# Unread products in front of four waits of TensorE in a one-core decoder layer

## Chip, cores and metric

The kernel runs on one core of a Trainium2 chip. The metric is the device time of one execution in microseconds (us). An engine's busy time, waits and the clock granted to TensorE (1.00 is the full 2.4 GHz, 0.50 is 1.2 GHz) come from one profiled execution.

## What is computed

One decoder layer on x of 512 tokens by 1024, float32. Two head groups read one combined projection; their outputs go through one output projection, then a LayerNorm, a routed mixture of experts and a second LayerNorm:

```python
def reference(x, w_in, ...):
    h = x
    p = h @ w_in
    p_rwkv, p_moba = p[..., :RWKV_COLS], p[..., RWKV_COLS:]
    p_prev = jnp.pad(p_rwkv[:, :-1], ((0, 0), (1, 0), (0, 0)))
    p_rwkv = p_rwkv + (p_prev - p_rwkv) * mu_shift
    p_r, p_k, p_v, p_wd, p_ad, p_gd = _split(p_rwkv, RWKV_SPLITS)
    y_a = _rwkv7_group(p_r, p_k, p_v, p_wd, p_ad, p_gd, ...)   # 8 recurrent heads x 64, delta rule
    q_m, k_m, v_m = _split(p_moba, MOBA_SPLITS)
    y_b = _moba_group(q_m, k_m, v_m)                            # 8 heads x 64, block-sparse attention
    mix = jnp.concatenate([y_a, y_b], axis=-1) @ w_out
    h = _layer_norm(DEEPNORM_ALPHA * h + mix, ln1_g, ln1_b)
    ffn = _hier_moe(h, ...)     # 4 groups, best 1; its 8 experts, best 2; SwiGLU, width 256
    h = _layer_norm(DEEPNORM_ALPHA * h + ffn, ln2_g, ln2_b)
```

## The kernel before

The engines are TensorE (PE; its weight loads are PEld), VectorE (DVE), ScalarE (ACT), GpSimdE (POOL) and SyncE (SP), which issues most loads. The code is written in stages; a scheduler sets each engine's order from priorities and estimated times, and each engine then runs its list strictly in that order. Where `strict[0]` is set, every product of TensorE is bound behind the one written before it; `last[1]` holds the product behind which the next ones are bound, `last[0]` the latest one written. `mm` (line 229) and `tp` (line 232) issue every product and transpose of TensorE, so nearly all its work bears one of these two lines, and is told apart by its banks (`bank0` to `bank7`, the eight accumulators; in the orders below `bank_64` to `bank_71`) and shapes. A float32 product of which both sides are full float32 shows as two pieces in the trace.

**Recurrent heads, 0 to 300 us.** The eight heads are worked in four pairs. For pair `hp`, `feat` makes the features. Its three projections (`proj`, of K, R and V) are 24 products of 128x512 each over hi and lo parts of x and of the weights; `split_w` makes these parts on ScalarE (line 336) and on VectorE or GpSimdE (line 337). Between K and R the norm of K is taken: four products with `hsel` into `pn`, the inverse root on VectorE and GpSimdE (`rsqrt`, lines 239 to 247, the last step on ScalarE), then four transposes into `pi`, which VectorE L441 reads. R is evacuated by L348 (ScalarE) and L349 (VectorE) and multiplied by GpSimdE L464; V is evacuated by L471 and L472. `pre` builds the pair's chunk matrices: its products of 128x128 need L464's result; VectorE masks them (lines 565 to 573) and solves a triangular system by 15 rounds of shuffle, product and sum (L578, L579, L580), after which TensorE goes on (`both`). `feat(1)` is woven into `pre(0)` by priority, and so on.

**Routing, about 430 to 490 us.** Token blocks 3 to 0 of 128 tokens are routed in an order written out by hand (`MODE`): output projection, transposes, logits, choice of experts (`picks`), position in the expert's list (`rank`: products of the blocks' masks, into bank 6), norm. `rows0` gathers the rows of the first expert pair with products of one-hot masks (128x128); then come `slots_of` (tables of places), `ups(0)` (32 products of the first pair's up weights), `gates_of` (the gate values, 128x32, for which VectorE and GpSimdE compute lines 1068 to 1086) and `read_gates`. `gains1` (lines 1007 and 1012) applies the LayerNorm's gain and bias on GpSimdE and VectorE beside it. SyncE stores the routing tables (line 1281) and behind that issues the next expert weights.

**Experts, about 490 to 755 us.** 32 experts are worked in 16 pairs (`experts_first`, `last_pair`), 64 rows each: `ups`, `hidden`, `turn`, `down`. Pairs 0 to 12 write to DRAM; from pair 13 (`LATE_`) on, `combine` adds the result to the tokens with one-hot products. Weights come through seven large and six small buffers; a load is issued when its buffer comes free. After the last pair comes the second LayerNorm.

Of the kernel before, what the change touches and what calls it, by code (L numbers as in the profile page):

```python
# [10 lines left out]
BF = mybir.dt.bfloat16  # L11
# [160 lines left out]
def v3(ap, a):  # L172
    return ap.rearrange("p (a b) -> p a b", a=a)
# [12 lines left out]
def layer(ctx: ExitStack, tc: tile.TileContext, xT, xt, wb, wad, pc, wla, al, gl, cst, cst2, cst3, abias, wout,  # L186
# [7 lines left out]
    B = [pps.tile([128, 512], F32, name=f"bank{i}") for i in range(8)]  # L194
# [9 lines left out]
    def bank(ids):  # L204
        k = rot.get(ids, 0)
        rot[ids] = k + 1
        return B[ids[k % len(ids)]]
# [4 lines left out]
    last = [None, None]  # L212
# [5 lines left out]
    strict = [False]  # L218
# [9 lines left out]
    def mm(o, l, r, start=True, stop=True):  # L228
        return inorder(PE.matmul(o, l, r, start=start, stop=stop, skip_group_check=True))  # L229

    def tp(o, i):
        return inorder(PE.transpose(o, i, late("ident")))  # L232

# [3 lines left out]
    def rsqrt(out, y, x, t):  # L237

        V.tensor_scalar(t.bitcast(I32), x.bitcast(I32), 1, None, op0=OP.logical_shift_right)
        V.tensor_scalar(y.bitcast(I32), t.bitcast(I32), -1.0, float(0x5F3759DF), op0=OP.mult, op1=OP.add)  # L240
        P.tensor_scalar(x, x, -0.5, None, op0=OP.mult)
        for j in range(3):
            P.tensor_tensor(t, y, y, op=OP.mult)
            P.tensor_tensor(t, t, x, op=OP.mult)
            P.tensor_scalar(t, t, 1.5, None, op0=OP.add)
            P.tensor_tensor(y, t, y, op=OP.mult)
        S.activation(v3(out, 8), y[:, :, None].to_broadcast([128, 8, 64]), AF.Copy)  # L247
# [151 lines left out]
    def feat(hp, fill=()):  # L399
# [34 lines left out]
        nx = T(24)  # L434
        V.tensor_scalar(nx.f[:, 0:8], pn[:, 0:8], 1e-24, None, op0=OP.max)
        rsqrt(kkn.f, nx.f[:, 8:16], nx.f[:, 0:8], nx.f[:, 16:24])
        pi = bank(LB)
        for i in range(4):
            tp(pi[:, 128 * i:128 * i + 128], kkn.f[:, 128 * i:128 * i + 128])
        nx.free()  # L440
        V.scalar_tensor_tensor(kkn.f, k.f, pcol(f"kk{hp}"), pi, op0=OP.mult, op1=OP.mult)  # L441
        at("fe", hp)
# [599 lines left out]

    def rank(i, lg4, mx, oo, gg, og, gm, ww, ww8, ex4, e2, gs, m4, r1, rr):
        prk = B[RKB][:, 0:32]
        for j in range(3, i, -1):
            mm(prk, onesb, mb[:, j, :], start=(j == 3), stop=False)
        mm(prk, trisb, mb[:, i, :], start=(i == 3))
        V.scalar_tensor_tensor(r1, v3(prk, 4), 1.0, m4, op0=OP.add, op1=OP.mult)
        V.tensor_reduce(rr[:, 0:8], r1.rearrange("p g e -> p e g"), axis=AX.X, op=OP.add)
        for e in range(2):  # L1050
            ins = V.tensor_scalar(OHP[i].f[:, 64 * e:64 * e + 64], late("iota64"), rr[:, e:e + 1], og[:, 0:1],
                                  op0=OP.is_equal, op1=OP.mult)
        placed[0] = ins
        return lg4, mx, oo, gg, og, gm, ww, ww8, ex4, e2, gs
# [95 lines left out]
    def ups(p, ht, ph):  # L1150

        for k in range(8):
            for e in range(2):
                ins = mm(ph[64 * e:64 * e + 64, :], v3(ht.f, 8)[:, k, 64 * e:64 * e + 64],
                   wa_[2 * p + e][:, 512 * k:512 * k + 512], start=(k == 0), stop=(k == 7))
        return ins
# [3 lines left out]
        gates(i, *kept[i], part=1)  # L1160

    strict[0], last[1] = True, ins
    ins = ups(0, HT, B[0])
    strict[0], last[1] = False, None
    for i in range(3, -1, -1):
        gates_of(i, rrs[i], OHt[i], ins)
# [109 lines left out]
    def experts_first():  # L1276


        for i in range(4):
            gains1(i, (P, V), True, (0,) if f"g{i}" in MODE else range(2))  # L1280
        after(SP.dma_start(rdram, RR.f), g1, "rows first")
        BB[6] = area("b6")
        GA.append(T(1024, BB[6]))
        HTs.append(T(1024, BB[6]))
        P.memset(GA[1].f, 0.0)
        gather(2)
        strict[0], last[1] = True, last[0]

        def second(p):
            Y = YY[p % 2]  # L1290
            for n in range(2):
                py = B[4 + n]
                down(p, n, py)
                if n:
                    V.tensor_copy(Y.g[:, 512:1024], py)
                else:
                    S.activation(Y.g[:, 0:512], py, AF.Copy)
            P.indirect_dma_start(out=ydram, out_offset=bass.IndirectOffsetOnAxis(ap=IDY.i[:, p:p + 1], axis=0),  # L1298
                                 in_=Y.g, in_offset=None, bounds_check=1023, oob_is_err=False)
            loads_b(p)  # L1300

        for p in range(15):
            ph = B[6] if p % 2 and p < LATE_ else B[0]
            if p:
                ups(p, HTs[p % 2], ph)
            if p == 13:
                L2.append(area(f"a{SA[4]}"))
                G2 = T(2048, L2[0])
                for j in range(2):
                    SP.dma_start(G2.f[:, 1024 * j:1024 * j + 1024], lnp[2 + j:3 + j, :].to_broadcast([128, 1024]))  # L1310
                P.tensor_scalar(G2.f[:, 0:1024], G2.f[:, 0:1024], -12.0 * K_ ** 5, None, op0=OP.mult)
                L2.append(G2)
            late_a = []
            if p < HP:
                load_pair(2 * p + 7, 7)
            for e in range(2 * p + 7, min(2 * p + 9, 2 * LQ) if p >= HP else 0):
                if p < 4 or e == 2 * p + 7:
                    load_a(e, SA)
                else:
                    late_a.append(e)  # L1320
            hidden(p, ph)
            if p < LATE_:
                rows(p + 1, dst=HTs[(p + 1) % 2])
                if p + 3 < 16:
                    gather(p + 3)
                if p > 0:
                    second(p - 1)
                if p == LQ - 3:
                    load_pair(2 * LQ, 0)
                turn(B[3])  # L1330
            else:
                cbs = lambda k: combine(p - 1, CBS[k]) if p > LATE_ else None
                if p == LATE_:
                    second(p - 1)
                    combining()
                    back()
                cbs(0)
                turn(B[3])
                cbs(1)
                py = bank((4, 5))  # L1340
                down(p, 0, py)
                parts(0, py)
                cbs(2)
                rows(p + 1, (0,), HTs[(p + 1) % 2])
                cbs(3)
                rows(p + 1, (1,), HTs[(p + 1) % 2])
                if p + 3 < 16:
                    gather(p + 3)
                ot(p)
                py = bank((4, 5))  # L1350
                down(p, 1, py)
                parts(1, py)
            for e in late_a:
                load_a(e, SA)
        gained_rows()
        last_pair(SB, None)
# [253 lines left out]
```

## Time and profile before

| | |
|---|---|
| median of 3 runs | 757.5 us (754.66 to 757.62) |
| the profiled execution | 756.99 us, span 754.9 us |
| mean granted clock of TensorE | 0.931 |
| busy: TensorE, VectorE, ScalarE, GpSimdE | 87%, 48%, 36%, 28% |
| bytes moved | 147.18 MB |

The span runs from the first to the last instruction; some 2 us of the profiled execution lie outside it. A row of work by time gives start, busy time, engine, line, operation, what is written and read, shapes and count, and in brackets the idle time of the engine ahead of it with what ended that time. A busy TensorE is not TensorE at its peak.

### The profile page before, as it was taken

To read this page: it belongs to the slowest core of one execution; us is meant where nothing else is said; L and a number is where in the kernel's file an instruction comes from. 1 tells how busy PE (TensorE), PEld (TensorE's weight loads), DVE (VectorE), ACT (ScalarE), POOL (GpSimd) and SP (SyncE) were. 2 spreads that over 40 slices of the span, in tenths; PEclk is the share of its full clock that TensorE was granted. 3 is DMA by queue.
4 is the path that set the end of the run, shared out by engine and by line. 5 is a ranking of instruction groups with operands and counts; after the bars stand their busy time and mean duration, and the time that the engine had idled before them with its cause. 6 is when DMAs were issued, how large, how long until landed. Compare 5 with 4: busy or idle time off the path is not lost.

```text
span 754.9 us, 9697 instructions
## 1 busy us (share of the span) xinstructions
PE 660.1 (87%) x3420; PEld 416.7 (55%) x3420; DVE 359.1 (48%) x1091; ACT 273.0 (36%) x581; POOL 211.4 (28%) x302
## 2 busy tenths in 40 slices
PE   8879999889998997979999997599999897779780
PEld 3757887688777876845675676333334232323240
DVE  4277258415841585236445587922121121103975
ACT  4344543544274444536424532223131131101330
POOL 4233553445345533110000041721111111101432
PEclk9979999999999999998989997899999998988985
DMA  9611011001100110465440467499999999999503
GB/s 327 233 56 57 29 56 57 28 29 57 57 29 28 53 46 1 140 238 173 156 158 38 153 237 282 165 358 420 423 426 423 425 421 425 425 417 410 227 2 115
DMA packets 28484, 147.18 MB, mean 195 GB/s; under 512 B 5114, under 2 KB 5626, under 8 KB 20493
## 3 DMA queue, kind: packets, MB, share of 16 engines
q1 hardware_dynamic: 23676, 134.61, 45.5%
q0 software_dynamic: 4608, 11.62, 3.9%
q8 instruction: 29, 0.48, 0.3%
q10 hardware_dynamic: 144, 0.26, 0.1%
q14 instruction: 27, 0.21, 0.1%
HBM read 138.38 MB, written 15.36 MB: 204 GB/s over the span
## 4 chain that ended last, share of the span: by engine, by line
PE 30%; DMA 18%; DVE 8%; POOL 2%; issue 1%; ACT 0%; SPq 0%; DVEq 0%; POOLq 0%; ACTq 0%
PE bank L229 26%; DMA b<-in_wex 17%; PE bank L232 4%; DVE a L147 2%; DVE base L1375 1%; DMA b<-hdram,base 1%; DVE x L1075 1%; DVE base L1204 1%; DVE base L147 1%; POOL base L1007 0%; DVE base L778 0%; POOL base L1012 0%; DVE a L1431 0%; DVE x L1226 0%; POOL x L1086 0%
## 5 line engine op out<-in xcount | busy, mean ns | idle before, releaser
L229 PE MATMUL bank<-a,b 128*128 128x512 f32 (+2 forms) x1112 | 308.7, 467 | 14.9 <-DMA a<-in_wex 12.3
L229 PEld LDWEIGHTS bank<-a,b 128*128 128x128 f32 (+1 forms) x1112 | 159.7, 177 | 94.7 <-issue 47.2
L229 PE MATMUL bank<-b,base 128*64 128x512 f32 (+1 forms) x412 | 93.4, 497 | 8.6 <-DMA b<-in_wex 6.9
L229 PE MATMUL bank<-a,base 128*64 128x512 f32 (+3 forms) x308 | 73.5, 560 | 1.2 <-DMA a<-in_wex 0.8
L337 POOL TENSOR_TENSOR b<-b,b 128x1024 fp32r<-128x1024 f32 x22 | 52.3, 2376 | 73.6 <-ACT b L336 64.6
L229 PEld LDWEIGHTS bank<-b,base 128*64 128x64 f32 (+1 forms) x412 | 42.4, 161 | 49.5 <-issue 34.2
L229 PE MATMUL bank<-a 128*128 128x128 f32 (+6 forms) x264 | 62.7, 370 | 7.2 <-ACT a L627 3.8
L1209 DVE SCALAR_TENSOR_TENSOR base<-bank,base 128x256 f32<-128x256 f32 x16 | 7.7, 483 | 116.9 <-ACT base L1208 116.9
L1208 ACT ACTIVATE base<-bank 128x256 f32<-128x256 f32 x16 | 6.1, 384 | 121.8 <-PE bank L229 121.8
L229 PEld LDWEIGHTS bank<-a 128*128 128x128 f32 (+2 forms) x264 | 37.9, 200 | 20.6 <-issue 6.1
L229 PEld LDWEIGHTS bank<-a,base 128*64 128x64 f32 (+2 forms) x308 | 27.3, 140 | 39.0 <-issue 27.2
L229 PE MATMUL bank<-a,a 128*128 128x128 f32 (+2 forms) x200 | 43.2, 334 | 2.1 <-POOL a L464 2.1
L232 PE MATMUL bank<-base,a 128*128 128x128 f32 x152 | 33.1, 298 | 9.5 <-ACT a L247 7.8
L229 PEld LDWEIGHTS bank<-a,a 128*128 128x128 f32 x200 | 33.2, 202 | 9.5 <-issue 3.7
L229 PE MATMUL bank<-base 128*128 128x36 f32 (+4 forms) x136 | 30.2, 365 | 6.7 <-DVE base L1040 3.3
L336 ACT ACTIVATE b<-b 128x1024 fp32r<-128x1024 f32 x25 | 26.3, 1057 | 26.1 <-PE bank L229 18.7
L232 PE MATMUL bank<-base 128*128 128x128 f32 x156 | 31.1, 302 | 5.1 <-DVE base L1209 3.9
L232 PEld LDWEIGHTS bank<-base 128*128 128x128 f32 x156 | 19.0, 149 | 27.9 <-issue 16.3
L232 PEld LDWEIGHTS bank<-base,a 128*128 128x128 f32 x152 | 19.3, 148 | 22.4 <-ACT a L247 8.9
L229 PE MATMUL bank<-b,a 128*128 128x128 f32 x192 | 31.4, 276 | 0.2 <-DVE a L633 0.2
L229 PEld LDWEIGHTS bank<-b,a 128*128 128x128 f32 x192 | 29.9, 191 | 2.7 <-DVE a L633 0.4
L1298 POOL DMA_INDIRECT ydram<-x,base x13 | 13.1, 1008 | 63.9 <-ACT base L1214 34.6
(302 smaller groups left out, 960.5 us busy)
## 6 DMA issues: line engine op xcount, KB each, us to landing
a<-in_wex SPq DMA_DIRECT2D x28, 2048.0 KB, 24.0
b<-in_wex SPq DMA_DIRECT2D x30, 1024.0 KB, 26.4
b<-in_wb SPq DMA_DIRECT2D x25, 512.0 KB, 3.3
a<-in_wex SPq DMA_DIRECT2D x16, 512.0 KB, 15.7
ydram<-base SPq DMA_DIRECT2D x1, 4096.0 KB, 15.1
a<-ydram POOLq DMA_DIRECT2D x4, 1024.0 KB, 16.0
x<-in_wout SPq DMA_DIRECT2D x6, 512.0 KB, 4.3
a<-in_xT SPq DMA_DIRECT2D x8, 256.0 KB, 5.0
```

Source lines behind the costliest of these rows:

```text
L147: ins = f(*args, **kw)
L229: return inorder(PE.matmul(o, l, r, start=start, stop=stop, skip_group_check=True))
L232: return inorder(PE.transpose(o, i, late("ident")))
L336: S.activation(hi.f, raw.f, AF.Copy)
L337: (V if 0 < k < 4 else P).tensor_tensor(lo.f, raw.f, hi.g, op=OP.subtract)
L1075: V.scalar_tensor_tensor(ww[:, :, 0], ww[:, :, 0], gs, og, op0=OP.mult, op1=OP.mult)
L1204: V.scalar_tensor_tensor(hb[:, i, ns], hb[:, i, ns], 1.0, pc_, op0=OP.mult, op1=OP.add, accum_out=SUM.f[:, 2 * i + n:2 * i + n + 1] if p = ...
L1208: S.activation(hd.f, ph[:, 0:256], AF.Silu)
L1209: V.scalar_tensor_tensor(hd.f, ph[:, 256:512], GT.f[:, p:p + 1], hd.f, op0=OP.mult, op1=OP.mult)
L1298: P.indirect_dma_start(out=ydram, out_offset=bass.IndirectOffsetOnAxis(ap=IDY.i[:, p:p + 1], axis=0), in_=Y.g, in_offset=None, bounds_chec ...
L1375: E.tensor_tensor(h, h, RT[i].f[:, 1024 * r + 512 * n:1024 * r + 512 * n + 512], op=OP.add)
```

## The change

A helper `keep(n, o)` issues n products of 128x128 by 128x512 in bf16, read from two constants (the identity and a ramp, taken as bf16 bits), into a bank whose content nobody needs at that time. Nothing reads the result. It is called at four places: ahead of the four transposes of the first pair of heads (8 products, bank 6), ahead of the rank products of token block 0 (9, bank 5), behind `ups(0)` and ahead of the gate products (14, bank 7), and in expert pair 13 behind `turn` and ahead of `down` (16, bank 7). At the first two places the products, and what is written behind them up to the transposes or the rank product, are also bound into the written order.

```diff
+    def keep(n, o):
+
+        for _ in range(n):
+            ins = mm(o, late("ident").bitcast(BF)[:, 0:128], late("iota512").bitcast(BF)[:, 0:512])
+        return ins
+
...
         rsqrt(kkn.f, nx.f[:, 8:16], nx.f[:, 0:8], nx.f[:, 16:24])
+        if hp == 0:
+            strict[0], last[1] = True, last[0]
+            keep(8, B[6])
         pi = bank(LB)
         for i in range(4):
             tp(pi[:, 128 * i:128 * i + 128], kkn.f[:, 128 * i:128 * i + 128])
+        strict[0], last[1] = False, None
         nx.free()
...
         prk = B[RKB][:, 0:32]
+        if i == 0:
+            strict[0], last[1] = True, last[0]
+            keep(9, B[5])
         for j in range(3, i, -1):
             mm(prk, onesb, mb[:, j, :], start=(j == 3), stop=False)
         mm(prk, trisb, mb[:, i, :], start=(i == 3))
+        strict[0], last[1] = False, None
...
     strict[0], last[1] = True, ins
-    ins = ups(0, HT, B[0])
+    ups(0, HT, B[0])
+    ins = keep(14, B[7])
     strict[0], last[1] = False, None
...
                 cbs(1)
+                if p == 13:
+                    keep(16, B[7])
                 py = bank((4, 5))
                 down(p, 0, py)
```

The scheduler places the new products, and moves other work with them. On TensorE in the first pair of heads, from the four norm products (128x2, into `bank_67`) to the four transposes (line 232, into `bank_66`), there stood before:

```order
L229 MATMUL bank_67<-x_88,a_1_77 128x2 x4
L229 MATMUL bank_64<-a_1_74,b_1_81 128x512 x2
L229 MATMUL bank_67<-x_88,a_1_77 128x130 x2
L229 MATMUL bank_64<-a_1_75,b_1_81 128x512
L229 MATMUL bank_64<-a_1_74,b_1_81 128x512 x2
L229 MATMUL bank_64<-a_1_75,b_1_81 128x512
L229 MATMUL bank_64<-a_1_74,b_1_81 128x512 x2
L229 MATMUL bank_64<-a_1_75,b_1_81 128x512
L229 MATMUL bank_64<-a_1_74,b_1_81 128x512
L232 MATMUL bank_66<-base,a_1_77 128x128 x4
```

Now the eight unread products (into `bank_70`, each with its weight load) stand behind the norm products; from the last of them on the list reads as follows (the transposes are now line 238):

```order
L229 LDWEIGHTS base
L229 MATMUL bank_70<-base 128x512
L229 MATMUL bank_67<-x_88,a_1_77 128x130 x2
L229 MATMUL bank_64<-a_1_74,b_1_81 128x512 x2
L238 MATMUL bank_66<-base,a_1_77 128x128 x4
L229 MATMUL bank_64<-a_1_75,b_1_81 128x512
L229 MATMUL bank_64<-a_1_74,b_1_81 128x512 x2
L229 MATMUL bank_64<-a_1_75,b_1_81 128x512
L229 MATMUL bank_64<-a_1_74,b_1_81 128x512
L229 MATMUL bank_66<-x_88,a_1_77 128x130 x2
```

Of the ten products of R (into `bank_64`) ahead of the transposes, eight moved behind them. On VectorE in the same pair, from the last masks of `pre(0)` to the rounds of the solution, there stood before (L568, L572 and L573 are masks, L472 and L476 belong to V):

```order
L572 TENSOR_TENSOR b_1_84<-bank_70,x_88 128x4x64
L578 STREAM_SHUFFLE base<-base 128x8x15
L579 TENSOR_TENSOR base<-base 128x8x15
L580 TENSOR_TENSOR base<-base 128x8x15
...
L580 TENSOR_TENSOR base<-base 128x8x13
L568 TENSOR_TENSOR base<-bank_68,x_88 128x512
L472 SCALAR_TENSOR_TENSOR a_1_78<-bank_65,base,a_1_77 128x8x64
L573 TENSOR_TENSOR b_1_84<-bank_68,x_88 128x4x64
L476 TENSOR_TENSOR a_1_78<-bank_67,a_1_78 128x512
L578 STREAM_SHUFFLE base<-base 128x8x12
```

and now (the lines' numbers are ten higher from line 472 on: L482 is V's evacuation, L578 and L583 are masks, L588 to L590 a round):

```order
L482 SCALAR_TENSOR_TENSOR a_1_78<-bank_65,base,a_1_77 128x8x64
L578 TENSOR_TENSOR a_1_80<-bank_70,x_88 128x512
L486 TENSOR_TENSOR a_1_78<-bank_67,a_1_78 128x512
L578 TENSOR_TENSOR base<-bank_68,x_88 128x512
L582 TENSOR_TENSOR b_1_84<-bank_70,x_88 128x4x64
L583 TENSOR_TENSOR b_1_84<-bank_68,x_88 128x4x64
L588 STREAM_SHUFFLE base<-base 128x8x15
L589 TENSOR_TENSOR base<-base 128x8x15
L590 TENSOR_TENSOR base<-base 128x8x15
```

V's evacuation moved from behind the third round to ahead of the first. On TensorE in the routing, from the second half of the last logits (128x36) to the rank product of block 0 (the fourth 128x32, into `bank_70`), there stood before:

```order
L229 MATMUL bank_71<-base 128x36 x4
L229 LDWEIGHTS base
L229 MATMUL bank_70<-base 128x32
...
L229 MATMUL bank_66<-x_2753,base 128x128 x2
L229 MATMUL bank_67<-x_2753,base 128x128 x4
L229 LDWEIGHTS base
L229 MATMUL bank_70<-base 128x32
```

and now, with nine unread products into `bank_69` between the first two kinds:

```order
L229 MATMUL bank_71<-base 128x36 x4
L229 LDWEIGHTS base
L229 MATMUL bank_69<-base 128x512
...
L229 LDWEIGHTS base
L229 MATMUL bank_70<-base 128x32
L229 MATMUL bank_66<-x_2761,base 128x128 x2
```

The six gather products (into `bank_66` and `bank_67`) moved from ahead of the rank product to behind it. At the third and fourth places nothing but the new products moved on TensorE. Around 472 to 490 us VectorE and GpSimdE also take the steps of the gates and gains in a slightly other order: one gain step of VectorE (line 1007) comes ahead of its work on the gathered rows, and GpSimdE takes its first L1084 after two gain steps instead of three.

## Rows read from the trace of the kernel before

**Rows 1.** The chain that ended last, in order of time: start, us, what.

```profile
553.69 30.05 DMA b<-in_wex
...
650.08 31.91 DMA b<-in_wex
682.03 3.28 PE bank L229 x6
```

**Rows 2.** TensorE's work by time, 24 to 60 us.

```profile
23.89 6.64 PE L229 MATMUL bank<-a,b 128*128 128x512 f32 x28
...
36.25 1.12 PE L232 MATMUL bank<-base,a 128*128 128x128 f32 x4 [1.97 <-ACT a L247]
37.02 1.63 PE L229 MATMUL bank<-a,b 128*128 128x512 f32 x3
...
43.56 1.22 PE L229 MATMUL bank<-a,a 128*128 128x128 f32 x4 [2.13 <-POOL a L464]
...
52.22 6.89 PE L229 MATMUL bank<-a,b 128*128 128x512 f32 x22 [2.52 <-DVE b L337]
```

**Rows 3.** Windows: us, busy PE PEld DVE ACT POOL (counts), clock, DMA share, GB/s.

```profile
36.00:37.00 1.00, 0.75 (x4) 0.75 (x5) 0.00 (x0) 0.20 (x1) 0.00 (x0) 0.63 0.00 0
...
53.00:54.00 1.00, 1.00 (x5) 0.77 (x4) 1.00 (x4) 0.00 (x0) 0.00 (x0) 0.66 0.76 246
```

**Rows 4.** TensorE's work by time, the kernel's first products.

```profile
1.44 4.34 PE L229 MATMUL bank<-base 128*128 128x512 bf16 x10 [1.44 <-DVE base L321]
```

**Rows 5.** GpSimdE's and VectorE's work by time, 28 to 62 us.

```profile
41.81 1.70 POOL L464 TENSOR_TENSOR a<-a 128x512 f32<-128x512 f32 x1
...
48.91 3.25 DVE L337 TENSOR_TENSOR b<-b,b 128x1024 fp32r<-128x1024 f32 x1
...
58.43 0.27 DVE L580 TENSOR_TENSOR base<-base 128x104 f32<-128x104 f32 x1
...
60.72 0.75 DVE L472 SCALAR_TENSOR_TENSOR a<-bank,base,a 128x512 f32<-128x512 f32 x1
```

**Rows 6.** VectorE's and TensorE's work by time, 74 to 92 us.

```profile
74.29 0.17 DVE L580 TENSOR_TENSOR base<-base 128x8 f32<-128x8 f32 x1
...
85.16 1.16 PE L229 MATMUL bank<-a 128*128 128x128 f32 x8 [1.58 <-ACT a L627]
```

**Rows 7.** TensorE's work by time, 455 to 474 us.

```profile
467.01 2.89 PE L229 MATMUL bank<-x,base 128*128 128x128 f32 x12
469.71 0.20 PE L229 MATMUL bank<-base 128*128 128x32 bf16 x1
...
471.79 2.02 PE L229 MATMUL bank<-x,base 128*128 128x128 f32 x16 [1.24 <-DVE x L920]
```

**Rows 8.** Windows in the routing.

```profile
459.00:460.00 1.00, 1.00 (x8) 1.00 (x8) 1.00 (x4) 0.00 (x0) 0.00 (x0) 0.75 1.03 442
...
469.00:470.00 1.00, 0.92 (x6) 0.77 (x5) 0.55 (x5) 0.00 (x0) 0.00 (x0) 0.63 0.50 184
```

**Rows 9.** All engines' work by time, 474 to 500 us.

```profile
475.67 4.74 DVE L1075 SCALAR_TENSOR_TENSOR x<-x 128x4 f32<-128x4 f32 x1
...
476.63 2.52 POOL L1007 TENSOR_TENSOR base<-base,b 128x512 f32<-128x512 f32 x2
...
489.07 0.37 PE L229 MATMUL bank<-x 128*128 128x32 bf16 x8 [7.57 <-POOL x L1084]
489.18 0.33 SPq L1281 DMA_DIRECT2D rdram<-x  x1
```

**Rows 10.** A window behind the second pair's up products.

```profile
499.00:500.00 1.00, 0.68 (x4) 0.00 (x0) 0.00 (x0) 0.25 (x1) 0.00 (x0) 1.00 0.37 140
```

**Rows 11.** TensorE's work by time, 655 to 760 us.

```profile
678.60 1.94 PE L229 MATMUL bank<-b,base 128*64 128x512 f32 x2 [5.39 <-DMA b<-in_wex]
682.03 3.28 PE L229 MATMUL bank<-b,base 128*64 128x512 f32 x6 [1.49 <-DMA b<-in_wex]
```

**Rows 12.** A window behind the fourth place.

```profile
684.00:685.00 1.00, 1.00 (x3) 0.02 (x1) 0.00 (x0) 0.00 (x0) 1.00 (x3) 0.61 1.07 414
```

## The prediction

> **What bounds the kernel now.** I read four views in this order: the page's table of engines, the chain that ended last, TensorE's work by time, and the granted clock in windows of 1 us. TensorE is the busiest engine, so a reader may think that every microsecond of it counts. The chain says otherwise for the second half: from 553.69 to 682.03 its links are loads of expert weights, each behind the one before, and only at 682.03 does it come back to TensorE [rows 1]. So a gain of TensorE between about 500 and 680 us is worth nothing, while a shift of the moment at which that stream of loads starts is worth itself. The stream starts behind SyncE's store at 489.18, which waits for the last gate values; the same values release TensorE at 489.07 after 7.57 us [rows 9]. Before 553 the chain is TensorE, VectorE and GpSimdE in turn, so the first and the second place of the change lie on the path, the third only through what follows it, and the fourth lies in front of a weight load.
>
> The clock is the reason for such products. It fell soon after waits of 1.97 and 2.52 us: the windows that straddle 36 and 53 us show 0.63 and 0.66, a fall from 2.4 to 1.2 GHz inside them [rows 2, 3]. It did not fall after 1.24 us at 471.79 [rows 7]. So the question at each place is how much idle time is left after the products.
>
> **The price of one product.** It is 128 rows by 512 columns. At the full clock 28 products of this width took 6.64 us, 0.237 us each [rows 2]. At the start of the kernel ten bf16 products of just this shape took 4.34 us, 0.434 us each [rows 4]. Between these two, 8, 9, 14 and 16 cost 1.9 to 3.5, 2.1 to 3.9, 3.3 to 6.1 and 3.8 to 6.9 us of TensorE. [...]
>
> **First place, first pair of heads (8 products).** Before, ten products of the projection of R stood between the four norm products and the four transposes, and TensorE then idled 1.97 us for ScalarE L247 [rows 2]. Now eight unread products and two of R stand there: again ten of 512 columns, so TensorE runs dry at the same moment, the wait is again about 2 us, and the transposes still start near 36.25. The clock has the same reason to fall. The eight themselves cost nothing, since the wait covers them; without that wait they would cost 1.9. What costs is what they push behind the transposes: eight products of R, 1.9 us at the full clock, and 4.3 at the 0.54 each that three took at 37.02 [rows 2].
>
> Step by step. R ends 1.9 to 4.3 us later. GpSimdE L464 needs it and releases the first product of the recurrence at 43.56 [rows 2, 5]; L464 ran straight behind other work of its engine, so part of the delay is slack: I take 2.5. Next, V's projection waits 2.52 us for VectorE's L337, 48.91 to 52.16 [rows 2, 5]. In the new order three steps of some 0.6 us that stood ahead of L337 come behind it, so V goes on 2.5 - 1.8 + 0.5 for the order of the rest = 1.2 us later, at 53.4. V's 6.89 us lay half at the low clock [rows 2, 3]; TensorE is now busier just ahead of it, so it may run at the full clock throughout: 0 to -1.7.
>
> Third, VectorE. Before, nine of the 45 steps of the substitution (three rounds, the last ending with L580 at 58.43) ran while V was still being computed, and V's evacuation L472 came at 60.72 [rows 5]. Now L472 stands ahead of all 45. The nine, about 0.3 us each, move behind it: 2.8 us, and two more steps come between, 1.2 us. The last L580, at 74.29 [rows 6], moves by 4.0 plus V's own shift (-0.5 to +1.2). Of this TensorE sees less: three projection products now stand ahead of the work that waits for it (0.7 us), and the wait of 1.58 us at 85.16 [rows 6] takes up the rest, about 1.6. That leaves 1.7 at V unchanged. After that TensorE has no gap of this size in the stage that would take it up. The term: -1.7 if other work covers the chain and V runs at the full clock, +4.3 if all of it passes. I take **+1.5**, nearer the upper half since the idle time that lets the clock fall is left as it was.
>
> **Second place, the routing of the first token block (9 products).** The clock was low from 459 to 469 us [rows 8]. The nine stand where the row at 467.01 starts (six products of the row gather, 2.89 us), ahead of the rank product that ran at 469.71 when its mask was ready [rows 7]. At the low clock nine end at 470.9, 1.2 us late; at the full one at 469.1, in time. Value +0.5. The six products go behind the rank product and are covered by the wait of 1.24 us before 471.79 and the 0.5. The order of the other engines moves too: VectorE takes one gain step (0.7 us) ahead of work that leads to the gather, +0.3; GpSimdE takes two instead of three large steps (1.26 us each) ahead of a small one that needs VectorE. VectorE's L1075, four columns wide, was held 4.74 us, over those large steps [rows 9]; one step fewer is 1.2 us sooner, less 0.4 for a longer pause: -0.8. [...] Term: -1.3 to +1.9, I take **0**.
>
> **Third place, behind the first pair's up products (14).** TensorE idles 7.57 us until 489.07 [rows 9]. At the full clock 3.3 us of it are filled and over 4 us stay empty, more than any wait after which the clock fell [rows 2]; even at the low clock 6.1 us fit. So nobody waits longer, and the clock is low again at 489. If it were not, the second pair would end sooner and the weight queue, at a share of 0.37 around 499.5 [rows 10], would lose less: at most 1.0. Term -1.0 to 0, taken **0**.
>
> **Fourth place, the fourteenth pair (16).** TensorE idles 5.39 us for weights until 678.60, runs two products, and idles again until 682.03 for the next load [rows 11]. The products fill 3.8 of the first wait; 1.6 us, two products and 1.49 us of waiting remain, about 3 us nearly empty, and the loads come when they come. After 682.03 the low clock lasts to 684.6 [rows 12]; half of that, 1.3, is the most that a kept clock gives. At the low clock sixteen would end at 680, covered by the load of 682.03. Term -1.3 to 0, taken **0**.
>
> **Sum.** The profiled execution took 756.99 us (span 754.9), 0.5 below the median 757.5. 757.0 + 1.5 + 0 + 0 + 0 = **758.5**.
>
> **Rivals.** (a) Faster: the clock is kept at all four places. Price: half of the 3.4 us stretches behind 36.3 and 53.3 (1.7 each), 0.8 in the routing, 1.0 and 1.3 at the last two: 6.5 us, **750.5**. For it: the products lie just in front of waits after which the clock fell. Against: in three of the four enough idle time remains. It decides if the remaining waits no longer let the clock fall. (b) Slower: the substitution on VectorE. If V ends after about 59 us, all 4.0 us of its shift plus V's 1.2 pass to TensorE, whose order is fixed, and the rank product is 1.2 late: 757.0 + 6.4, less 0.7 for the products moved ahead, **762.7**. For it: VectorE was full through this stretch. Against: the wait at 85.16. (c) The change does not do what it says: products placed ahead of a wait leave the remaining wait as long as before, so that the clock falls where it fell. That is part of the forecast, for the first, third and fourth places.
>
> **Chances.** Forecast with its own terms (754 to 761): 0.56. Rival (a), wholly or for the front alone: 0.24. Rival (b): 0.20. About 0.5% (3.8 us) is what a measurement here tells from no change; so faster 0.24, same 0.56, slower 0.20. The range for 8 in 10 runs from 751.5 to 762.5: it takes in most of (a) and of (b).
>
> **What would show it.** In the changed profile: the transposes near 36.25 with a wait of about 2 us ahead of them and a fall of the clock after it (if none, the first place works); L472 ahead of the first shuffle, and the last L580 near 78 instead of 74.29; the wait at 85.16 gone; the rank product up to 1.2 us later; the gate products near 489 at the low clock; a fall of the clock before 682. The forecast is wrong if the clock stays full at 36 and 53 us, or if TensorE at 135 us is later than before by over 4 us.

## The result: slower by 0.65%

The changed kernel took 761.3 us in the median of 11 runs (759.04 to 764.85), the kernel before 755.65 us in the same comparison. The ratio is 1.0065 with a 95% interval of 1.0039 to 1.0091, so 4.9 us (2.9 to 6.9) were lost. A second comparison, with the same two kernels, gave 1.0038 (1.0002 to 1.0073). The forecast was 758.5 us, 751.5 to 762.5, with "no change" as the likeliest case; the measured time lies in the range, near its slow end. The prediction took 0.5% as the least that tells a change from none; by that, the first comparison is a slowdown, to which it gave a chance of 0.20, and the second falls short of it.

The profiled execution of the changed kernel took 763.88 us, span 761.9 us, mean granted clock 0.929. Its chain that ended last has the same shape as [rows 1]: loads of expert weights, and TensorE behind the last of them, about 7 us later. Columns: start, us, what.

```profile
568.33 33.81 DMA a<-in_wex
...
689.35 3.68 PE bank L229 x6
```

So the delay was there when the weights began to stream. It arose earlier, and the first stage shows its first part. TensorE's work by time in the changed kernel (start, busy time, engine, line, operation, shapes, count, idle time ahead and what ended it; L253 and L474 are L247 and L464 of before):

```profile
31.46 1.89 PE L229 MATMUL bank<-base 128*128 128x512 bf16 x8
...
33.55 0.71 PE L229 MATMUL bank<-a,b 128*128 128x512 f32 x2
36.44 0.66 PE L238 MATMUL bank<-base,a 128*128 128x128 f32 x4 [2.18 <-ACT a L253]
...
44.25 2.08 PE L229 MATMUL bank<-a,a 128*128 128x128 f32 x8 [3.04 <-POOL a L474]
...
50.67 5.25 PE L229 MATMUL bank<-a,b 128*128 128x512 f32 x22
```

Against [rows 2]: the eight products cost nothing by themselves, and the wait ahead of the transposes is as long as before (2.18 against 1.97). The wait for R's product on GpSimdE grew from 2.13 to 3.04. V's projection no longer waits and runs in 5.25 instead of 6.89 us: it begins 1.55 us earlier and ends 3.2 earlier. Then VectorE (L482 is V's evacuation, L590 the sum of a round of the substitution, L640 a transposition of its outcome):

```profile
57.63 0.76 DVE L482 SCALAR_TENSOR_TENSOR a<-bank,base,a 128x512 f32<-128x512 f32 x1
...
75.38 0.17 DVE L590 TENSOR_TENSOR base<-base 128x8 f32<-128x8 f32 x1
...
76.72 0.71 DVE L640 STREAM_TRANSPOSE a<-a 128x512 f32<-128x512 f32 x1 [1.17 <-POOL a L621]
```

and TensorE in the same stretch:

```profile
74.38 1.18 PE L229 MATMUL bank<-a,b 128*128 128x512 f32 x4
77.49 2.08 PE L229 MATMUL bank<-a 128*128 128x128 f32 x8 [1.93 <-DVE base L441]
...
86.54 1.16 PE L229 MATMUL bank<-a 128*128 128x128 f32 x8 [1.46 <-ACT a L637]
```

A wait of 1.93 us stands at 77.49 that the kernel before does not have. The row names L441, but these products read the output of L640, which ended at 77.43. The clock fell in that wait. Windows (us, busy PE, PEld, DVE, ACT, POOL with counts, clock, DMA share, GB/s):

```profile
57.00:76.00 19.00, 17.98 (x95) 13.76 (x93) 16.86 (x69) 11.92 (x26) 6.63 (x4) 1.00 0.17 56
76.00:82.00 6.00, 4.51 (x26) 4.46 (x27) 2.06 (x7) 1.19 (x2) 5.70 (x9) 0.72 0.00 1
```

The products at 86.54 are the ones that stood at 85.16 in [rows 6]. They serve as the **landmark** below: behind them TensorE is busy for all of the next 40 us (40.84 of 40.84 from 85.16 us in the kernel before, 40.00 of 40.00 from 86.54 here), so no idle time there takes up a delay. Against the first trace of before the delay at the landmark is only 1.4 us. The other 5.6 us of the two spans came later, most of it in attention (TensorE 2.7 us late at 340 us, 9.0 at 360), where all engines have the order of before and the clock stayed low far longer:

```profile
341.00:350.00 9.00, 8.36 (x32) 5.32 (x33) 5.08 (x12) 4.80 (x11) 1.27 (x1) 0.50 0.52 181
350.00:360.00 10.00, 10.00 (x29) 4.61 (x29) 3.85 (x11) 3.31 (x10) 0.00 (x0) 0.50 0.46 143
```

In the kernel before, the clock was 0.67 and 1.00 in these two windows. One pair of traces can't tell whether that belongs to the change, so it was a question for the experiments.

### The profile page after: what moved, and what is told of

Its sections match the earlier page's. It is cut to its first block, busy times and chain, and to the rows that moved or that the text cites. A ratio compares the mean times of both kernels' runs of the same rounds, so it can differ in the third digit from the quotient of the medians.

```text
span 761.9 us, 9792 instructions
## 1 busy us (share of the span) xinstructions
PE 675.5 (89%) x3467; PEld 420.1 (55%) x3467; DVE 354.1 (46%) x1091; ACT 272.3 (36%) x581; POOL 210.0 (28%) x302
## 4 chain that ended last, share of the span: by engine, by line
PE 35%; DMA 14%; DVE 9%; POOL 1%; ACT 1%; issue 1%; DVEq 0%; POOLq 0%; ACTq 0%; SPq 0%
PE bank L229 31%; DMA a<-in_wex 9%; DMA b<-in_wex 4%; PE bank L238 4%; DVE a L147 1%; DVE base L1392 1%; DMA b<-hdram,base 1%; DVE base L1219 1%; DVE base L147 1%; DVE x L1089 0%; DVE base L1022 0%; DVE x L1098 0%; POOL base L1022 0%; DVE base L788 0%; DVE a L1448 0%
## 5 line engine op out<-in xcount | busy, mean ns | idle before, releaser
L343 POOL TENSOR_TENSOR b<-b,b 128x1024 fp32r<-128x1024 f32 x22 | 52.3, 2377 | 72.9 <-ACT b L342 72.7
L229 PE MATMUL bank<-a 128*128 128x128 f32 (+6 forms) x264 | 64.5, 380 | 8.2 <-ACT a L637 3.7
L229 PEld LDWEIGHTS bank<-a,base 128*64 128x64 f32 (+2 forms) x308 | 24.7, 140 | 42.9 <-issue 33.8
L229 PE MATMUL bank<-base 128*128 128x36 f32 (+4 forms) x183 | 40.8, 370 | 6.5 <-DVE base L1050 3.7
L1313 POOL DMA_INDIRECT ydram<-x,base x13 | 13.1, 1009 | 62.8 <-ACT base L1229 42.3
```

The lines of the kernel that those rows point to most:

```text
L343: (V if 0 < k < 4 else P).tensor_tensor(lo.f, raw.f, hi.g, op=OP.subtract)
```

## The experiments

In the expectations, theory A says that the first place carries the loss, B the routing, C that only the positions of the clock's falls differ. A1 puts the loss on VectorE's order, A2 on R's products or the unread ones. Where the recorded texts write 2.4 and 1.2 GHz, the profile gives shares, 1.00 and 0.50 of the full clock: the unread products of the changed kernel start 0.215 us apart at 1.00 (31.46 to 32.97 us) and 0.427 at 0.50 (474.81 to 477.80 us), that is 2.4 and 1.2 columns per ns.

**Each place alone.** The first: eight products and the binding in `feat(0)`.

```diff
+        if hp == 0:
+            strict[0], last[1] = True, last[0]
+            keep(8, B[6])
         pi = bank(LB)
```

> Only the first place is changed (8 products and the binding). Theory A, the first place carries the slowdown (R's products behind the transposes, VectorE's substitution later; TensorE was 0.7 us late at 100 us and 9.0 us late at 380 us in the changed kernel): 4 to 6 us over the kernel before, ratio 1.005 to 1.008, transposes near 36.4 after a wait of about 2.2 us, a wait of about 1.9 us at 77 us. Theory B, the routing carries it: within 1.5 us of before. Theory C, the changed kernel only met other positions of the clock's falls between 100 and 400 us, where the order of all engines is as before: TensorE 0.7 us late at 100 us, then any shift between -2 and +8 us at 400 us by the clock, and a median within 2 us of before.

Measured: 760.36 us, ratio 1.0041 (1.0010 to 1.0073). The new wait is there (1.93 us at 78.76), and the landmark is at 87.81, 2.65 us later than in [rows 6]; theory C had TensorE 0.7 us late at 100 us. Here the clock stayed full at the new wait and fell at the landmark (0.66 in the last window):

```profile
78.76 1.16 PE L229 MATMUL bank<-a 128*128 128x128 f32 x8 [1.93 <-DVE base L441]
87.81 2.07 PE L229 MATMUL bank<-a 128*128 128x128 f32 x8 [2.67 <-ACT a L637]
```

```profile
76.00:82.00 6.00, 4.07 (x30) 3.42 (x29) 2.71 (x11) 2.02 (x5) 4.96 (x5) 1.00 0.00 1
87.00:92.00 5.00, 4.19 (x18) 3.85 (x19) 0.00 (x0) 1.84 (x4) 0.10 (x1) 0.66 0.00 0
```

The first place alone loses 3.1 us (0.8 to 5.5), less than the 4 to 6 expected by theory A, and about two thirds of the 4.9 of all four; the intervals overlap. The second place: nine products ahead of the rank products of block 0.

```diff
+        if i == 0:
+            strict[0], last[1] = True, last[0]
+            keep(9, B[5])
```

> Only the second place is changed (9 products and the binding in the routing). Theory A: within 1 us of before; rank product 0 to 1.3 us later against the products ahead of it, as in the changed kernel, and taken back by the first weight store (VectorE and GpSimdE steps as in the changed kernel). Theory B: 3 to 5 us over before, seen as a later store. Theory C: within 1 us.

Measured: 757.29 us, ratio 0.9996 (0.9964 to 1.0028). TensorE in the routing, first of this kernel, then of the one with the third place alone, which has the routing of before (the first row merges eight products of the last logits, the nine unread ones and four rank products of block 0):

```profile
462.96 5.55 PE L229 MATMUL bank<-base 128*128 128x36 f32 x21
...
468.89 0.26 PE L229 MATMUL bank<-base 128*128 128x32 bf16 x4
...
470.39 2.02 PE L229 MATMUL bank<-x,base 128*128 128x128 f32 x16 [0.26 <-DVE x L926]
...
486.44 0.38 PE L229 MATMUL bank<-x 128*128 128x32 bf16 x8 [6.33 <-POOL x L1094]
```

```profile
467.21 0.23 PE L229 MATMUL bank<-base 128*128 128x32 bf16 x1
467.80 0.26 PE L229 MATMUL bank<-base 128*128 128x32 bf16 x4 [0.36 <-DVE x L1054]
469.30 2.02 PE L229 MATMUL bank<-x,base 128*128 128x128 f32 x16 [1.24 <-DVE x L926]
...
478.66 3.19 PE L229 MATMUL bank<-base 128*128 128x512 bf16 x14
...
486.57 0.38 PE L229 MATMUL bank<-x 128*128 128x32 bf16 x8 [4.53 <-POOL x L1090]
```

The next rank products are 1.1 us later (468.89 against 467.80; 0.2 of it was there before the routing) and the row gather as well, and the wait of 1.24 us shrinks to 0.26. At the gate products the two kernels stand within 0.13 us of each other, so the delay was given back, and most of it where the prediction had looked for it: the four-column step of VectorE that lasted over GpSimdE's large steps (L1075 of before: 4.74 us up to 480.41, GpSimdE's up to 480.38; the same step took 0.21 us at 480.60) took 3.53 us with the second place (first line) and 4.71 without it. It began 1.57 us later and ended 0.39 later.

```profile
474.75 3.53 DVE L1085 SCALAR_TENSOR_TENSOR x<-x 128x4 f32<-128x4 f32 x1
473.18 4.71 DVE L1081 SCALAR_TENSOR_TENSOR x<-x 128x4 f32<-128x4 f32 x1
```

Theory B falls.

The third and fourth places, `ins = keep(14, B[7])` behind `ups(0)` and `keep(16, B[7])` in pair 13:

> Only the third place is changed (14 products ahead of the gate products). All theories: nobody waits for these products, within 1 us of before; the clock is low for 3 to 4 us before the gate products instead of 10 us, and the first pair's steps after it gain at most 1 us.

> Only the fourth place is changed (16 products in expert pair 13). The weight loads decide this stretch, so within 1 us of before, with the clock's fall before 682 us still there (6.8 us at 1.2 GHz). If the products held up the weight stream, 1 to 3 us slower.

Measured: 757.69 us, ratio 1.0011 (0.9976 to 1.0047), and 756.55 us, ratio 1.0014 (0.9980 to 1.0047). In the last row above, 4.53 us of idle time are left behind the fourteen products, and the clock fell in them all the same:

```profile
482.00:485.00 3.00, 0.04 (x2) 0.00 (x0) 2.97 (x4) 0.00 (x0) 3.00 (x4) 0.99 0.00 0
485.00:488.00 3.00, 1.43 (x14) 1.43 (x14) 2.48 (x8) 0.04 (x1) 2.94 (x5) 0.50 0.16 53
```

At the fourth place, TensorE by time and then the clock, in the kernel with that place alone:

```profile
672.86 3.62 PE L229 MATMUL bank<-base 128*128 128x512 bf16 x16
678.38 1.04 PE L229 MATMUL bank<-b,base 128*64 128x512 f32 x2 [1.90 <-DMA b<-in_wex]
681.85 3.68 PE L229 MATMUL bank<-b,base 128*64 128x512 f32 x6 [2.43 <-DMA b<-in_wex]
```

```profile
681.00:685.00 4.00, 3.15 (x6) 0.76 (x6) 0.49 (x1) 0.00 (x0) 2.20 (x4) 0.50 0.98 393
```

The loads come when they came, within 0.3 us of [rows 11], and the clock is low at 682, as before. It stayed full through the first wait (1.00 from 676 to 681), where before lost it at 678 (0.50 from 678 to 684), and fell in the second, at 681.

**The last three together, without the first.**

> Places two, three and four without the first. If the first place carries the change: within 1.5 us of before (757). If the small amounts of the three alone (0.0, +0.8 and +1.1 us by their ratios, none clear of zero) are real and add: 1.9 us over before.

Measured: 757.05 us, ratio 0.9991 (0.9958 to 1.0024). The small excesses of the third and fourth place alone do not add up to anything that the time shows. The trace has one more thing to tell: its front is that of before, and yet its clock was low in attention from 335.7 to 359.6 us, just as in the first trace of the changed kernel:

```profile
341.00:350.00 9.00, 9.00 (x31) 4.85 (x29) 4.44 (x11) 3.72 (x10) 0.00 (x0) 0.50 0.46 145
350.00:360.00 10.00, 10.00 (x34) 4.80 (x34) 3.35 (x13) 3.86 (x12) 0.00 (x0) 0.52 0.30 100
```

**Both kernels once more.**

> The changed kernel once more, for a second trace and more times: 4 to 6 us over before as measured; TensorE 2 to 6 us later at 100 us than in the kernels with places 2, 3 or 4 alone; and if the 24 us at 1.2 GHz near 340 to 364 us of its first trace were chance, 10 to 14 us there now.

> The kernel before once more, for a second trace. If the three falls of the clock (36.3, 43.1, 53.3 us) in its first trace were a matter of position: TensorE 1.5 to 2.7 us earlier at 100 us, as in the four kernels that have its front; the last round of the substitution at 71.8 to 72.6 us instead of 74.5.

Measured: the changed kernel 760.2 us, ratio 1.0038 (1.0002 to 1.0073), which is 2.9 us and less than the 4 to 6 expected; the kernel before 1.0003 (0.9959 to 1.0047) against itself. In the second trace of the changed kernel the landmark is at 87.93, and the second of the two windows in attention is at 0.78 instead of 0.50:

```profile
341.00:350.00 9.00, 7.35 (x30) 4.53 (x30) 4.21 (x8) 3.91 (x9) 1.95 (x5) 0.50 0.54 178
350.00:360.00 10.00, 10.00 (x42) 5.21 (x42) 4.95 (x19) 4.98 (x13) 0.00 (x0) 0.78 0.54 179
```

So the long low stretch came once in two traces of the changed kernel, and also in a kernel with the front of before: it is no effect of the change that these traces could show, and it had made the first pair of spans differ by more than the medians do. In the second trace of before the landmark is at 84.11, 1.05 us earlier than in [rows 6]; less than the 1.5 to 2.7 expected, and the last round came at 73.24 and not by 72.6: V's projection took 6.91 us there, about as long as in the first trace (6.89), and 5.28 to 5.32 in the four kernels with places 2, 3, 4 or these three together.

**VectorE's order alone.** No unread product; a dependency binds the first shuffle of the first pair's substitution behind V's evacuation.

```diff
-        V.scalar_tensor_tensor(ar[:, :, 128:192], c8(ps), ...)
+        d["ve"] = V.scalar_tensor_tensor(ar[:, :, 128:192], c8(ps), ...)
...
-            V.stream_shuffle(zt3[:, :, s + 1:], ...)
+            sh = V.stream_shuffle(zt3[:, :, s + 1:], ...)
+            if hp == 0 and s == 0:
+                after(sh, d["ve"], "order")
```

> The kernel before without any unread product; only VectorE's substitution of the first pair is bound behind V's evacuation, as it stands in the changed kernel. Theory A1, this order is what the first place costs: last round of the substitution at 75 to 77 us instead of 71.8 to 72.6 (the kernels with places 2, 3 or 4 alone), a new wait of TensorE of 1 to 2 us near 77 us, and 2 to 4 us over before. Theory A2, the products of R behind the transposes, or the products themselves, cost it: within 1 us of before.

Measured: 759.33 us, ratio 1.0034 (0.9990 to 1.0078). The interval just reaches 1, so its time alone does not settle it. The trace is clearer. TensorE, ScalarE and GpSimdE do their work in the order of before, and only VectorE's order differs; yet TensorE and the clock show:

```profile
77.40 1.98 PE L229 MATMUL bank<-a 128*128 128x128 f32 x8 [2.23 <-DVE a L632]
85.96 1.16 PE L229 MATMUL bank<-a 128*128 128x128 f32 x8 [0.29 <-ACT a L629]
```

```profile
76.00:82.00 6.00, 4.60 (x25) 4.51 (x26) 1.97 (x6) 1.68 (x5) 5.59 (x9) 0.72 0.01 1
```

The new wait (here with the right releaser, the transposition), the fall at it and a landmark later than in all six traces with the front of before appear without a single unread product.

**The products without that order.** The first place with its eight products, and V's evacuation (stage `fj` of pair 0) at a lower priority, so that VectorE takes two rounds of the substitution first.

```diff
-    PRI = {"ga2": 200, "ga1": -50}
+    PRI = {"ga2": 200, "ga1": -50, "fj0": -30}
```

> The first place alone with its eight products and the binding, but V's evacuation has a lower priority, so that VectorE again takes two rounds of the substitution ahead of it (three before, none with the first place alone). TensorE's order up to the transposes is that of the changed kernel. A1: last round near 72 to 74 us, no new wait at 77 us, within 1 us of before. A2: 2 to 4 us over before, as with the first place alone.

Measured: 756.55 us, ratio 0.9978 (0.9939 to 1.0018). The wait near 77 us is gone, and the landmark is at 83.68. The same line in the changed kernel, with all four places:

> All four places of the change, with V's evacuation of the first pair at a lower priority, so that VectorE takes two rounds of the substitution ahead of it. If VectorE's order is all that the change costs: within 1.5 us of before (ratio 0.997 to 1.002), 3 to 5 us below the changed kernel, last round of the substitution at 72 to 74 us. If the four places cost something by themselves when together: 2 to 4 us over before.

Measured: 756.6 us, ratio 1.0005 (0.9976 to 1.0034). VectorE, TensorE and the clock there:

```profile
56.98 0.74 DVE L482 SCALAR_TENSOR_TENSOR a<-bank,base,a 128x512 f32<-128x512 f32 x1
...
71.08 0.17 DVE L590 TENSOR_TENSOR base<-base 128x8 f32<-128x8 f32 x1
```

```profile
81.95 1.16 PE L229 MATMUL bank<-a 128*128 128x128 f32 x8 [1.57 <-ACT a L637]
```

```profile
76.00:82.00 6.00, 4.43 (x38) 4.11 (x36) 1.38 (x2) 1.84 (x5) 3.97 (x13) 1.00 0.29 91
```

One priority takes back the whole loss with every unread product in place. It gains nothing over the kernel before either. It moves more than VectorE's rounds: against the changed kernel, GpSimdE's L343, two steps of ScalarE (L457, L458) and some of TensorE's products also change places between 74 and 95 us. What VectorE's order does by itself is shown by the run with the order alone.

**Filling the wait, and leaving R where it was.** Sixteen products at the first place (with `"fi0": -60`, which keeps VectorE's order near that of before), and eight behind R's products (with higher priorities for R, `fg0` and `fh0`, and for the first pair's matrices, and a lower one for `fj0`).

```diff
-            keep(8, B[6])
+            keep(16, B[6])
```

> The first place alone with 16 instead of 8 products, V's projection of the first pair at a lower priority (four rounds of the substitution ahead of V's evacuation). If the fall of the clock behind the transposes comes from the wait that eight products leave: the wait falls from 2.2 to 0.3 to 0.7 us and the clock stays at 2.4 GHz from 36 to 42 us; R's products then come later, the wait for R on GpSimdE is 2.8 us or more, and the clock falls behind that instead, so that the time stays within 1.5 us of before. If the clock falls at 36 to 40 us in spite of it, its reason is not that wait.

> The first place alone with eight products, but R's products ahead of them (higher priority for R and for the first pair's matrices), so that R is not pushed behind the transposes. Transposes 1 to 2 us later (37.3 to 38.3 us), a wait of at most 1.3 us ahead of them, R's consumer on GpSimdE not later than in the kernels with places 2, 3 or 4 alone. Theory A1: last round of the substitution at 71 to 73 us and the time within 1.5 us of before, 1 us faster if the clock does not fall at 36 us.

Measured: 756.17 us, ratio 1.0016 (0.9978 to 1.0054), and 758.43 us, ratio 1.0004 (0.9968 to 1.0040). With sixteen:

```profile
36.40 0.66 PE L238 MATMUL bank<-base,a 128*128 128x128 f32 x4 [1.36 <-ACT a L253]
...
44.99 2.07 PE L229 MATMUL bank<-a,a 128*128 128x128 f32 x8 [2.94 <-POOL a L474]
```

The wait fell to 1.36 us, not to 0.3 to 0.7. The clock stayed full through 36 to 42 us (1.00) and fell at 44.9 (0.86 from 42 to 46 us), at the end of the 2.94 us of waiting for R. With R ahead the transposes came at 37.43 after 1.15 us, and the clock first fell at 44.0 (1.00 from 36 to 42 us, 0.75 from 42 to 46). Neither is clear evidence that the wait was what mattered, since the clock stayed full from 36 to 42 us also where the whole wait is there (1.00 behind 1.97 us in the second trace of before, last section). Neither is faster than the kernel before: no version here beats it.

## Why the prediction was right or wrong

All traces together, in three groups. "V" is the start of V's evacuation, "last" that of the last round's sum, both on VectorE.

| kernel | V | last | last - V | landmark | ratio |
|---|---|---|---|---|---|
| before | 60.72 | 74.29 | 13.57 | 85.16 | 1 |
| before, second trace | 59.69 | 73.24 | 13.55 | 84.11 | 1.0003 |
| second place | 58.88 | 72.38 | 13.50 | 83.25 | 0.9996 |
| third place | 58.67 | 72.14 | 13.47 | 83.01 | 1.0011 |
| fourth place | 58.22 | 71.66 | 13.44 | 82.53 | 1.0014 |
| second to fourth | 58.66 | 72.11 | 13.45 | 82.99 | 0.9991 |
| first, two rounds ahead | 58.71 | 72.81 | 14.10 | 83.68 | 0.9978 |
| all four, two rounds ahead | 56.98 | 71.08 | 14.10 | 81.95 | 1.0005 |
| sixteen | 61.02 | 73.25 | 12.23 | 84.13 | 1.0016 |
| eight behind R | 58.92 | 73.02 | 14.10 | 83.88 | 1.0004 |
| changed kernel | 57.63 | 75.38 | 17.75 | 86.54 | 1.0065 |
| changed, second trace | 59.04 | 76.75 | 17.71 | 87.93 | 1.0038 |
| first place | 58.92 | 76.65 | 17.73 | 87.81 | 1.0041 |
| order alone | 58.92 | 75.28 | 16.36 | 85.96 | 1.0034 |

The means of the landmark are 83.5 (front of before), 83.4 (unread products, rounds ahead of V) and 87.1 us (all rounds behind V). The last group is 3.6 us later at the landmark and 0.45% (3.4 us) slower in the mean of its ratios; nobody else is slower by more than 0.16%. The landmark accounts for the loss.

Two later marks bear on this. The last round of the second pair comes at 133.5 to 136.8 us in the first ten traces of the table and at 137.4 to 140.4 in the last four, 3.8 us later in the mean than with the front of before. That of the fourth pair comes at 291.2 to 294.0 us in the ten and at 296.1 to 297.1 in the three with unread products and all rounds behind V. With the order alone it comes at 293.7: still later than the six traces with the front of before, but among the four of the middle group. So the removal of the order takes the loss away, in two kernels and by their times; that the order alone, without the products, costs as much to the end of the kernel is not shown.

**First place, the wait itself: right.** Ten products of 512 columns stood ahead of the transposes as before, the transposes came at 36.44 after 2.18 us, and the products gained and cost nothing there.

**R: right.** The forecast was 2.5 us at the first product that waits for R. Against [rows 2] it came 0.7 us later in the first trace of the changed kernel, but 2.3 in the kernel with the first place alone (45.84) and 2.4 in the second trace (45.95). In these two the five products of R behind the transposes took 2.48 us, against 1.40 in the first trace; the clock of the second trace was 0.50 from 37 to 40 us.

**V: wrong, without consequence.** V's projection did not come 1.2 us later: it starts at 50.7, 51.9 and 52.0 us in the three traces with eight products and all rounds behind V, and at 51.2 to 52.2 in the six with the front of before. Its wait of 2.52 us for L337 shrank to 0.4 us or none. Its 5.25 us, at the full clock (1.00 from 53 to 54 us), are no gain of the change: it takes 5.28 to 5.32 us in four of the six traces with the front of before. The first trace of before, with 6.89 us, was a slow one at this place, and the latest of the six at the landmark, by 1.65 us above their mean. The sum stood on it; measured from it, the front of the changed kernel was only 0.7 to 3.6 us late 100 us into the kernel. The upper end of the front's term, 4.3, is 4.5 by its own parts (4.0 + 1.2 - 0.7).

**VectorE's shift: right.** The prediction had 4.0 us between V's evacuation and the last round; it is 4.2 (17.7 against 13.5).

**What TensorE sees of it: wrong, and this is the step that failed.** The prediction took 0.7 us off for the products moved ahead (they are there, at 74.38) and 1.6 for the wait at 85.16. That wait did not go; it is 1.46 at 86.54. It could not take anything up. From the last round's sum to the landmark pass 10.87 us, to within 0.01, in all ten traces where VectorE takes rounds ahead of V, and 10.7 to 11.2 in the other four. The two rows at 85.16 and 86.54 name ScalarE's copy (L627, now L637), and what held that copy was ScalarE's order: it stands behind the last step of the second pair's inverse root, which waited for GpSimdE. First before, then in the changed kernel:

```profile
77.40 0.34 DVE L435 TENSOR_SCALAR base<-bank 128x8 f32<-128x8 f32 x1
83.99 0.63 ACT L247 ACTIVATE a<-base 128x512 f32<-128x512 f32 x1 [3.70 <-POOL base L246]
```

```profile
77.36 0.13 DVE L441 TENSOR_SCALAR base<-bank 128x8 f32<-128x8 f32 x1
84.82 0.63 ACT L253 ACTIVATE a<-base 128x512 f32<-128x512 f32 x1 [3.25 <-POOL base L252]
```

VectorE begins this root only beside the two transpositions of the substitution's outcome (L630, now L640), behind the last round: in the changed kernel at 77.36, though its products on TensorE were done by 74.5. So the chain to the wait runs from the late step itself, through three engines, and moves as one. Slack belongs to a wait only if the late thing is not upstream of what it waits for. Instead a new wait of 1.9 us appeared at 77.5. It is the same delay, seen earlier, and no second one, nor did the fall of the clock at it hold up the landmark: 11.16 us pass in the first trace of the changed kernel, which has that fall, and 11.16 and 11.18 in the two traces of the same front without it. In these two the clock fell at the landmark instead (0.66 from 87 to 92 us, against 1.00 in the first trace), and some 1.2 us more went by behind it: 63.6 us between the last rounds of the first and the second pair, against 62.0 to 62.5 in the other twelve. The term was +1.5; against the kernels with the front of before it is 3.6 at the landmark.

**Second to fourth place: right.** The rank products came about a microsecond later and the store did not; nobody waited longer for the fourteen and sixteen products; the clock fell at both places, where 4.5 us, and 1.9 and 2.4 us, of idle time were left. Rival (c), that the remaining wait is as long as before, was so at the first place (2.18 against 1.97); at the third and fourth the products shortened it (4.5 us left of 7.57, 1.9 of 5.39), and the clock fell all the same, at the fourth at 681 us instead of 678. (In [rows 12] the 0.61 from 684 us on puts the end of the low clock at 684.8 and not at 684.6; half of the stretch is 1.4 and not 1.3, which changes no sum.)

**The rivals.** (a), the kept clock, did not happen: no kernel is clearly faster than before. (b) had the mechanism. Its condition, V done after about 59 us, was met only roughly (V's evacuation starts at 57.6 to 59.0), and its price of 6.4 us less 0.7 was too high by two, because it added V's 1.2 and the rank product's 1.2, neither of which passed. With the full shift as the only term the change would have been 4.0 - 0.7 = 3.3 us, between the two losses measured (4.9 and 2.9). The measured 761.3 lies just above the band that the forecast gave its own terms (754 to 761); the range held because it was stretched to take in most of (b).

**What would have shown it.** One test was badly chosen: "wrong if the clock stays full at 36 and 53 us". It did in the first trace (1.00 from 36 to 37 and from 53 to 54 us), and the kernel was still slower: the place of a fall changed between the executions of one kernel (42.9 us in its first trace, 37.0 in its second).

## What to carry over

Filler in front of a wait cost its own engine next to nothing here (the transposes came at 36.44 us against 36.25), but a scheduler that orders all engines by estimated times sees it as work and may turn another engine's order around, as it did here; compare every engine's order, and hold the order of the chain that matters by a priority or a dependency. Before a downstream wait is counted as slack, follow it back: if its releaser depends on the late step, be it only through the order of another engine, it moves along and absorbs nothing. Where the clock's falls wander, measure a stage by a landmark in several traces and not by one pair.

## What was not expected of the hardware

The same code with the same wait did not always lose the clock at the same place. Behind the wait of 1.97 us ahead of the transposes, the first trace of the kernel before shows 0.63 between 36 and 37 us [rows 3]. Its second trace, with the same wait, shows:

```profile
36.00:37.00 1.00, 0.74 (x6) 0.71 (x7) 0.00 (x0) 0.20 (x1) 0.00 (x0) 1.00 0.00 0
37.00:40.00 3.00, 2.01 (x13) 1.39 (x12) 2.33 (x4) 1.35 (x3) 0.68 (x1) 1.00 0.00 0
...
42.00:46.00 4.00, 3.48 (x11) 2.45 (x12) 1.77 (x2) 2.37 (x5) 1.38 (x2) 0.57 0.00 0
```

Here the clock fell only at 42.3. The changed kernel did the reverse, 42.9 in its first trace and, after the same 2.19 us of waiting, 37.0 in its second:

```profile
37.00:40.00 3.00, 3.00 (x11) 2.52 (x10) 0.75 (x1) 0.12 (x1) 0.10 (x1) 0.50 0.00 0
```

What sets the place was not shown. That it changes bears on the price of such products: a wait of this size was followed by the low clock within a microsecond in one execution (0.63 from 36 to 37 us) and not for six microseconds in another (1.00 from 36 to 42). How much is at stake is seen in attention, where one and the same order of instructions had the clock low for 10 us in the first trace of before and for 24 us in that of the changed kernel. Over these 20 us the changed kernel fell back by 6.2 us (from 2.7 late at 340 us to 9.0 at 360), of which 1.5 were back by 400 us. Even so it is more than the change itself.
